# A two-layer hybrid encoder on one core: gate rows through device memory, idle transposes with another term order, and roots by logarithm and exponential

## The chip, the cores and the metric

The kernel runs on one core of a Trainium2 chip. The metric is the time on the device in microseconds (us); lower is better. Before the change the median of three runs is 829.52 us (829.41 to 829.79). A core has five engines that run at the same time, each with its own list of instructions in a fixed order: TensorE (PE in the profile: matrix products and transposes, with its weight loads as PEld), VectorE (DVE), ScalarE (ACT: functions such as exponential, also plain copies), GpSimd (POOL) and SyncE (SP, which here only issues transfers). SyncE and ScalarE each issue transfers (DMAs) on a queue of their own. Data lies in device memory, in the on-chip memory of 128 partitions, and in eight accumulation banks that TensorE writes.

## The reference, cut to what matters

The sequence has 512 tokens of width 1024, all in 32-bit floats. Both layers have one frame; only the mixers differ.

```
ada = silu(c) @ ada_w + ada_b                  # one vector of 3072 for each layer
shift, scale, gate = split(ada, 3)
h = rmsnorm(x, norm_g) * (1 + scale) + shift   # rmsnorm: x * rsqrt(mean(x*x) + 1e-6) * g
... = split(h @ in_w)                          # layer 0: a, u, v, gate path; layer 1: q, k, v and more
y = concat(mixer 1, mixer 2) * silu(gate path)
x = x + gate * (y @ out_w)                     # the "gate row" is this vector gate, 1024 long
```

Layer 0 mixes by causal pooling and by a spatial gating; layer 1 by gated linear attention and by stick-breaking attention. A last `rmsnorm` ends the program.

## The kernel before, in words

**Precision.** Each 32-bit operand of a large product is split into a rounded high part (copied by ScalarE, line 185 or 190) and the remainder (subtracted by VectorE, line 186 or 191). `mm3` (lines 198 to 201) adds three products: high by high, high by low, low by high. A weight tile is 128x1024; four buffers take it raw, three take its two parts, and its load is issued by SyncE.

**Layout.** Activations `x` stand with tokens on the partitions, four blocks of 128 tokens. `h` is kept transposed, features on the partitions: eight tiles `h_hi`, `h_lo` of 128x512. Six of the eight accumulation banks have the tag "mm" and take the large products, two have the tag "aux".

**ada.** `ada_block` multiplies 128 rows of the transposed `ada_w` by `silu(c)` and sums along the row, so that one column of the tile `ada` (128x48) holds 128 values. Columns 16 to 23 of a layer's 24 are the gate.

**First phase.** `prepare_first` makes the norm of the four token blocks of `x`, transposes the first 128 features of each block (line 409) and makes the first `h` tile. After the transposes of blocks 1 to 3 `idle_work` runs 4 transposes of the identity each into a bank that is overwritten later (line 399). Then comes a loop over the eight feature tiles k. Each k has seven products, four for `v` (tokens on the partitions) and three for the gate path, which accumulate in seven banks over all k. For k = 0 all first terms are issued, then the preparation of the next `h` tile, then the second and third terms; for the others the three terms of a product follow each other. `prepare(k + 1)` transposes (line 314, in `modulate`), scales and splits the next `h` tile. After the loop `tok_evac` copies the `v` banks out (lines 466 and 468), and the next unit of products begins in the banks that become free.

**Gate rows.** The last product of a layer has tokens on the partitions, so the gate must lie along the row, the same in every partition, in a tile `gbc` of 128x1024 (line 354 multiplies by it). `gate_half` makes half of it: for four columns of `ada` VectorE spreads the column over a 128x128 tile `rep` (line 327), TensorE transposes it into an "aux" bank (line 332), and ScalarE copies the bank to `gbc` (line 333). For layer 0 `gate_rows(0)` stands ahead of the output product; for layer 1 the halves are set into the steps of the stick-breaking heads.

**Output product and norm.** `out_proj` makes the left 512 columns for all four token blocks, then the right 512 for blocks 0 and 1, and then for 2 and 3. Each evacuation multiplies by `gbc`, adds `x`, and lets ScalarE sum the squares of the half row (`square`, line 343) into a column of `ss`. After the first half it calls `mid`, after each pair of blocks `after`. In layer 0 `after` is `ln1`: `token_rstd` adds the two half sums on VectorE (line 369), GpSimd turns the sum into the mean (line 299) and raises it to the power -0.5 (line 300), and VectorE multiplies the block by the root (`normalise`, line 305); TensorE's transposes of the next layer's `modulate` wait for it. In layer 1 `after` is `final`, which already takes the root as exp(-0.5 ln(...)) on ScalarE (lines 969 and 970), with the first half's mean as the logarithm's bias. The function table for both is loaded in `mid`.

**Order.** A planner orders each engine's instructions by readiness, program order first among those that are ready, and adds the waits; it may start work far ahead of its place in the program. Where the code says `manual_schedule`, the named engine keeps the program's order: all three engines in `prepare_first`, TensorE in the first phase and in the attention part of layer 1, where `at` and `boundary` hang small pieces of work into the gaps between quarter units. Tiles of one tag are handed out in turn: "big" has five buffers of 128x1024, which the tiles `v`, `gbc`, `n`, `gv`, `sv` and `fg` share.

Of the kernel before, what the change touches and what calls it, by code (L numbers as in the profile page):

```python
# [9 lines left out]
F32 = mybir.dt.float32  # L10
F32R = mybir.dt.float32r
AF = mybir.ActivationFunctionType
ALU = mybir.AluOpType
PSUM = bass.MemoryType.PSUM

D = 1024
# [23 lines left out]
def pack_inputs(i):  # L40
# [12 lines left out]
    ng, ab = np.asarray(i["norm_g"]), np.asarray(i["ada_b"])  # L53
# [22 lines left out]
    for c in range(4):  # L76
# [6 lines left out]
        "adaT": f(np.asarray(i["ada_w"]).transpose(0, 2, 1).reshape(48, P, D)),  # L83
# [15 lines left out]
def trunk(ctx: ExitStack, tc: tile.TileContext, d, out):  # L99
# [5 lines left out]
    psum = ctx.enter_context(tc.tile_pool(name="psum", bufs=1, space=PSUM))  # L105
    uid = [0]
# [214 lines left out]
    def gate_half(l, n):  # L321

        reps = []
        for i in range(4):
            c = 24 * l + 16 + 4 * n + i
            reps.append(pool.tile([P, P], F32, name=nm("rep"), tag="diag", bufs=4))
            V.tensor_scalar(out=reps[i], in0=ones, scalar1=ada[:, c:c + 1], scalar2=None, op0=ALU.mult)

        def turn(g):
            ps = bank("aux")  # L330
            for i in range(4):
                T.transpose(ps[:, i * P:(i + 1) * P], reps[i], ident)
            A.copy(out=g[:, n * 512:(n + 1) * 512], in_=ps)
        return turn

    def gate_rows(l):
        g = big("gbc")
        for n in range(2):
            gate_half(l, n)(g)
        return g  # L340
# [4 lines left out]
    def out_proj(wo, y, gbc, ssc, after, mid, nxt):  # L345
# [19 lines left out]
        return late  # L365

# [34 lines left out]
    def prepare_first():  # L401
# [4 lines left out]
        for t in range(TB):  # L406
            if t == TB - 1:
                last_block(0, P)
            T.transpose(ps[:, t * P:(t + 1) * P], xn[t][:, :P], ident)
            idle_work(t and 4)  # L410
# [23 lines left out]
    with tc.manual_schedule(engines={T.engine}):  # L434
        with tc.manual_schedule(engines={V.engine, A.engine}):
            prepare_first()
        for k in range(KT):
            ops = list(first_products(k))
            if k:
                if k + 1 < KT:  # L440
                    prepare(k + 1)
                for o in ops:
                    mm3(*o, False, k == KT - 1)
                continue
            for ps, lh, ll, rh, rl in ops:
                T.matmul(ps, lh, rh, start=True, stop=False)
            prepare(1)
# [4 lines left out]
            for ps, lh, ll, rh, rl in ops[:TB]:  # L452
                T.matmul(ps, ll, rh, start=False, stop=False)
            for ps, lh, ll, rh, rl in ops[TB:]:
                T.matmul(ps, lh, rl, start=False, stop=False)
# [140 lines left out]
    def ln1(tbs):  # L596
        xn = {t: normalise(t, token_rstd(t, 16)) for t in tbs}

        def late():
            for k in range(KT):  # L600
                modulate(1, k, tbs, xn)
        return late
    pre = []

    def preload():
        pre.append(tc.keep_in_program_order(A.preload_act_table_set("natural_log_exp_and_others")))
# [300 lines left out]
    gbc, turns = big("gbc"), []  # L907
    wo1 = stream(d["wo1"])
    at(g0 + 2, lambda: turns.append(gate_half(1, 0)))
    at(g0 + 3, lambda: turns[0](gbc))  # L910
    at(g0 + 3, lambda: turns.append(gate_half(1, 1)))
    at(g0 + 5, lambda: turns[1](gbc))
# [43 lines left out]

    fg = big("fg")
    nc.sync.dma_start(out=fg, in_=d["fg"].to_broadcast([P, D]))

    def first_sum(t):  # L960

        s = sm("msq")
        V.tensor_scalar(out=s, in0=ss[:, 24 + 2 * t:25 + 2 * t], scalar1=1.0 / D, scalar2=EPS, op0=ALU.mult, op1=ALU.add)
        return s

    def final(tbs):
        for t in tbs:
            r = sm("rstd")
            A.activation(out=r, in_=ss[:, 25 + 2 * t:26 + 2 * t], func=AF.Ln, scale=1.0 / D, bias=msq[t])
            A.activation(out=r, in_=r, func=AF.Exp, scale=-0.5)  # L970
# [8 lines left out]
    msq = [None] * TB  # L979

    def scale_first():
        tc.keep_in_program_order(A.preload_act_table_set("natural_log_exp_and_others"))
        for t in range(TB):
            msq[t] = first_sum(t)
# [21 lines left out]
```

## Time and profile before

| What | Value |
|---|---|
| median of three runs | 829.52 us |
| the profiled execution's own time | 829.61 us |
| its span (first to last instruction) | 827.9 us |
| TensorE busy | 812.4 us, 98% of the span |
| VectorE busy | 510.1 us, 62% |
| ScalarE busy | 401.7 us, 49% |
| GpSimd busy | 55.0 us, 7% |
| moved by DMA | 108.50 MB, mean 131 GB/s |
| ScalarE's table loads | 4, of 1.28 us each |

A row of the timeline gives the start in us from the span's start, the duration, the engine, the line of the kernel, the operation, the tile written and the tiles read, shapes and the count of merged instructions. In brackets at its end stands how long the engine had been idle before it, and what released it. Matmuls overlap: the next one starts before the one before has ended, so their pace is read from starts. TensorE's transposes are listed as matmuls that read `ident`. A row of a group gives shortest, median and longest duration in ns and the first and the last start. A row of the DMA issues gives KB each and the us from issue to landing.

### The profile page before, as it was taken

To read this page: it belongs to the slowest core of one execution; us is meant where nothing else is said; L and a number is where in the kernel's file an instruction comes from. 1 tells how busy PE (TensorE), PEld (TensorE's weight loads), DVE (VectorE), ACT (ScalarE), POOL (GpSimd) and SP (SyncE) were. 2 spreads that over 40 slices of the span, in tenths; PEclk is the share of its full clock that TensorE was granted. 3 is DMA by queue.
4 is the path that set the end of the run, shared out by engine and by line. 5 is a ranking of instruction groups with operands and counts; after the bars stand their busy time and mean duration, and the time that the engine had idled before them with its cause. 6 is when DMAs were issued, how large, how long until landed. Compare 5 with 4: busy or idle time off the path is not lost.

```text
span 827.9 us, 9967 instructions
## 1 busy us (share of the span) xinstructions
PE 812.4 (98%) x3696; PEld 663.3 (80%) x3696; DVE 510.1 (62%) x806; ACT 401.7 (49%) x675; POOL 55.0 (7%) x122
## 2 busy tenths in 40 slices
PE   6999999999999999999999999999999999999996
PEld 4888888888888888778888888877777777888885
DVE  6856855588783377744664543475756568434885
ACT  5453321233243265653453423666767668552663
POOL 3000301100000000000000000011010101020000
PEclk9999999999999999999999999999999999999999
DMA  8977555554552235423222121222121212322362
GB/s 301 303 284 236 192 174 170 198 178 155 176 203 80 95 116 178 164 97 102 88 91 72 69 90 51 103 82 96 50 80 51 99 55 77 102 77 96 108 201 105
DMA packets 31298, 108.50 MB, mean 131 GB/s; under 512 B 3601, under 2 KB 3729, under 8 KB 31250
## 3 DMA queue, kind: packets, MB, share of 16 engines
q1 hardware_dynamic: 30674, 106.82, 38.5%
q10 hardware_dynamic: 576, 1.05, 0.3%
q8 instruction: 29, 0.48, 0.2%
q14 instruction: 19, 0.16, 0.1%
HBM read 105.76 MB, written 2.10 MB: 130 GB/s over the span
## 4 chain that ended last, share of the span: by engine, by line
PE 95%; DVE 2%; DMA 1%; ACT 1%; issue 1%; POOL 0%; SPq 0%; DVEq 0%; ACTq 0%
PE mm L200 27%; PE mm L201 27%; PE mm L199 27%; PE aux L848 2%; PE aux L883 2%; PE aux L875 1%; PE aux L529 1%; PE aux L759 1%; PE aux L314 1%; DMA x<-in_x 1%; PE aux L761 1%; PE aux L201 1%; PE aux L199 1%; PE aux L200 1%; PE aux L732 1%; PE aux L770 1%
## 5 line engine op out<-in xcount | busy, mean ns | idle before, releaser
L186 DVE TENSOR_TENSOR wlo<-raw,whi 128x1024 fp32r<-128x1024 f32 (+1 forms) x145 | 178.0, 1228 | 122.5 <-ACT whi L185 122.1
L185 ACT ACTIVATE whi<-raw 128x1024 fp32r<-128x1024 f32 (+1 forms) x145 | 152.4, 1051 | 205.7 <-PE mm L200 93.5
L199 PE MATMUL mm<-hhi,whi 128*128 128x512 f32 x566 | 229.7, 406 | 0.0
L201 PE MATMUL mm<-hhi,wlo 128*128 128x512 f32 x566 | 221.3, 391 | 0.0
L200 PE MATMUL mm<-hlo,whi 128*128 128x512 f32 x566 | 220.9, 390 | 0.0
L200 PEld LDWEIGHTS mm<-hlo,whi 128*128 128x128 f32 x566 | 106.6, 188 | 22.5 <-issue 1.9
L201 PEld LDWEIGHTS mm<-hhi,wlo 128*128 128x128 f32 x566 | 106.3, 188 | 22.8
L199 PEld LDWEIGHTS mm<-hhi,whi 128*128 128x128 f32 x566 | 106.5, 188 | 22.4 <-issue 1.9
L175 DVE CUSTOM_DVE_ANT_0 raw<-raw,sc,cols 128x1024 f32<-128x1024 f32 x48 | 61.4, 1283 | 47.1 <-DMA raw<-in_adaT 46.9
L199 PE MATMUL mm<-whi,hhi 128*128 128x512 f32 x188 | 75.8, 403 | 0.0
L201 PE MATMUL mm<-whi,hlo 128*128 128x512 f32 x188 | 73.9, 393 | 0.0
L200 PE MATMUL mm<-wlo,hhi 128*128 128x512 f32 x188 | 73.6, 391 | 0.0
L201 PE MATMUL mm<-whi,r 128*128 128x512 f32 x160 | 62.7, 392 | 0.0
L199 PE MATMUL mm<-whi,r 128*128 128x512 f32 x160 | 62.5, 392 | 0.0
L200 PE MATMUL mm<-wlo,r 128*128 128x512 f32 x160 | 62.5, 391 | 0.0
L201 PEld LDWEIGHTS mm<-whi,hlo 128*128 128x128 f32 x188 | 35.3, 188 | 7.5
L190 ACT ACTIVATE r<-y 128x256 fp32r<-128x256 f32 (+1 forms) x60 | 27.0, 479 | 29.2 <-PE mm L201 23.2
L191 DVE TENSOR_TENSOR r<-y,r 128x256 fp32r<-128x256 f32 (+1 forms) x60 | 29.1, 510 | 19.4 <-PE mm L200 16.5
L200 PEld LDWEIGHTS mm<-wlo,hhi 128*128 128x128 f32 x188 | 35.4, 188 | 6.9
L199 PEld LDWEIGHTS mm<-whi,hhi 128*128 128x128 f32 x188 | 35.4, 188 | 6.7
L200 PEld LDWEIGHTS mm<-wlo,r 128*128 128x128 f32 x160 | 30.1, 188 | 6.4 <-DVE wlo L186 0.3
L199 PEld LDWEIGHTS mm<-whi,r 128*128 128x128 f32 x160 | 30.1, 188 | 6.1
(222 smaller groups left out, 1052.4 us busy)
## 6 DMA issues: line engine op xcount, KB each, us to landing
raw<-in_w SPq DMA_DIRECT2D x89, 512.0 KB, 3.3
raw<-in_adaT SPq DMA_DIRECT2D x48, 512.0 KB, 4.3
raw<-in_wo SPq DMA_DIRECT2D x48, 512.0 KB, 3.3
raw<-in_wfirst SPq DMA_DIRECT2D x8, 448.0 KB, 4.4
x<-in_x SPq DMA_DIRECT2D x4, 512.0 KB, 5.3
kq<-in_poolw SPq DMA_DIRECT2D x4, 256.0 KB, 5.8
out<-x SPq DMA_DIRECT2D x4, 256.0 KB, 2.6
out<-x ACTq DMA_DIRECT2D x4, 256.0 KB, 2.8
```

The source lines that it names most:

```text
L175: V.tensor_tensor_reduce(out=t, in0=t, in1=sc, scale=1.0, scalar=cols[:, C_AB[l] + b:C_AB[l] + b + 1], op0=ALU.mult, op1=ALU.add, accum_ou ...
L185: A.activation(out=hi[:, :w], in_=t[:, :w], func=AF.Copy)
L186: V.tensor_tensor(out=lo[:, :w], in0=t[:, :w], in1=hi.bitcast(F32)[:, :w], op=ALU.subtract)
L190: A.activation(out=hi, in_=src, func=AF.Copy)
L191: V.tensor_tensor(out=lo, in0=src, in1=hi.bitcast(F32), op=ALU.subtract)
L199: T.matmul(o, lh, rh, start=start, stop=False)
L200: T.matmul(o, lh, rl, start=False, stop=False)
L201: T.matmul(o, ll, rh, start=False, stop=stop)
L314: T.transpose(ps[:, i * P:(i + 1) * P], xn[t][:, k * P:(k + 1) * P], ident)
L529: T.matmul(ps[:, t * P:(t + 1) * P], v[t][:, hd * P:(hd + 1) * P], sguw[hd // 4][:, c], start=True, stop=True)
L848: T.matmul(ps[:, c0:c0 + (t + 1) * P], q[:, t * P:(t + 1) * P], k[:, :(t + 1) * P], start=True, stop=True)
L883: T.matmul(ps[:, s * P:], sv[hd // 4][s][:, hd % 4 * P:(hd % 4 + 1) * P], wt[s], start=s == 0, stop=s == 3)
```

## The change

Three edits are made together.

Gate rows: `gate_half` goes. `gate_rows` stores the eight gate columns of `ada` to a row of device memory and loads that row into all partitions of `gbc`, both on ScalarE's queue. So that the store is contiguous in each partition, the host lays the gate rows of `ada_w` and `ada_b` in another order (`ada_rows`). The steps in the stick-breaking part go, and layer 1 calls `gate_rows(1)` after it.

First phase: `idle_work` runs 6, 7, 9 and 6 transposes after the transposes of blocks 0 to 3, where it ran 0, 4, 4 and 4; and all k use the order of terms that k = 0 had.

Second norm: `ln1` uses `quick_rstd`, the code of `final`, in place of `token_rstd`; `half_means` makes the first half's means of all four blocks in one instruction, for both layers.

```diff
+    def ada_rows(w):
+        return np.concatenate([w[:2 * D], w[2 * D:].reshape(P, 8, -1).transpose(1, 0, 2).reshape(D, -1)])
...
+    dram = ctx.enter_context(tc.tile_pool(name="dram", bufs=1, space=bass.MemoryType.DRAM))
...
-    def gate_half(l, n):
-        reps = []
-        for i in range(4):
-            c = 24 * l + 16 + 4 * n + i
-            reps.append(pool.tile([P, P], F32, name=nm("rep"), tag="diag", bufs=4))
-            V.tensor_scalar(out=reps[i], in0=ones, scalar1=ada[:, c:c + 1], scalar2=None, op0=ALU.mult)
-        def turn(g):
-            ps = bank("aux")
-            for i in range(4):
-                T.transpose(ps[:, i * P:(i + 1) * P], reps[i], ident)
-            A.copy(out=g[:, n * 512:(n + 1) * 512], in_=ps)
-        return turn
-
     def gate_rows(l):
         g = big("gbc")
-        for n in range(2):
-            gate_half(l, n)(g)
+        row = dram.tile([1, D], F32, name=nm("grow"))
+        c = ada[:, 24 * l + 16:24 * l + 24]
+        nc.scalar.dma_start(out=row.rearrange("o (p n) -> (o p) n", n=8), in_=c)
+        nc.scalar.dma_start(out=g, in_=row.to_broadcast([P, D]))
         return g
...
+    def half_means(ssc):
+        m = sm("msq", TB)
+        V.tensor_scalar(out=m, in0=ss[:, ssc:ssc + 2 * TB:2], scalar1=1.0 / D, scalar2=EPS, op0=ALU.mult, op1=ALU.add)
+        return m
+
+    def quick_rstd(t, ssc, m):
+        r = sm("rstd")
+        A.activation(out=r, in_=ss[:, ssc + 2 * t + 1:ssc + 2 * t + 2], func=AF.Ln, scale=1.0 / D, bias=m[:, t:t + 1])
+        A.activation(out=r, in_=r, func=AF.Exp, scale=-0.5)
+        return r
...
-            idle_work(t and 4)
+            idle_work((6, 7, 9, 6)[t])
...
             ops = list(first_products(k))
-            if k:
-                if k + 1 < KT:
-                    prepare(k + 1)
-                for o in ops:
-                    mm3(*o, False, k == KT - 1)
-                continue
+            if 0 < k < KT - 1:
+                prepare(k + 1)
             for ps, lh, ll, rh, rl in ops:
-                T.matmul(ps, lh, rh, start=True, stop=False)
-            prepare(1)
+                T.matmul(ps, lh, rh, start=k == 0, stop=False)
+            if k == 0:
+                prepare(1)
             for ps, lh, ll, rh, rl in ops[:TB]:
                 T.matmul(ps, lh, rl, start=False, stop=False)
             for ps, lh, ll, rh, rl in ops[TB:]:
                 T.matmul(ps, ll, rh, start=False, stop=False)
             for ps, lh, ll, rh, rl in ops[:TB]:
-                T.matmul(ps, ll, rh, start=False, stop=False)
+                T.matmul(ps, ll, rh, start=False, stop=k == KT - 1)
             for ps, lh, ll, rh, rl in ops[TB:]:
-                T.matmul(ps, lh, rl, start=False, stop=False)
+                T.matmul(ps, lh, rl, start=False, stop=k == KT - 1)
...
-        xn = {t: normalise(t, token_rstd(t, 16)) for t in tbs}
+        xn = {t: normalise(t, quick_rstd(t, 16, means[0])) for t in tbs}
...
     def preload():
-        pre.append(tc.keep_in_program_order(A.preload_act_table_set("natural_log_exp_and_others")))
+        means.append(half_means(16))
+        tc.keep_in_program_order(A.preload_act_table_set("natural_log_exp_and_others"))
...
-    at(g0 + 2, lambda: turns.append(gate_half(1, 0)))
-    at(g0 + 3, lambda: turns[0](gbc))
-    at(g0 + 3, lambda: turns.append(gate_half(1, 1)))
-    at(g0 + 5, lambda: turns[1](gbc))
...
+    gbc = gate_rows(1)
     fg = big("fg")
...
-            r = sm("rstd")
-            A.activation(out=r, in_=ss[:, 25 + 2 * t:26 + 2 * t], func=AF.Ln, scale=1.0 / D, bias=msq[t])
-            A.activation(out=r, in_=r, func=AF.Exp, scale=-0.5)
+            r = quick_rstd(t, 24, means[1])
```

More of the change, by code (lines that the diff above doesn't have):

```diff
@@ L51, in c_tiles @@
         return w[:, c0:c0 + 256].reshape(k, 4, P, 256).transpose(0, 2, 1, 3).reshape(k, P, 1024)
-    ng, ab = np.asarray(i["norm_g"]), np.asarray(i["ada_b"])
+    def ada_rows(w):
+        return np.concatenate([w[:2 * D], w[2 * D:].reshape(P, 8, -1).transpose(1, 0, 2).reshape(D, -1)])
+    ng, ab = np.asarray(i["norm_g"]), [ada_rows(b[:, None])[:, 0] for b in np.asarray(i["ada_b"])]
     cols = np.concatenate(
@@ L82, in pack_inputs @@
         "cols": f(cols),
-        "adaT": f(np.asarray(i["ada_w"]).transpose(0, 2, 1).reshape(48, P, D)),
+        "adaT": f(np.stack([ada_rows(w.T) for w in np.asarray(i["ada_w"])]).reshape(48, P, D)),
         "wfirst": f(first),
@@ L602, in ln1 @@
         return late
-    pre = []
+    means = []
     def preload():
-        pre.append(tc.keep_in_program_order(A.preload_act_table_set("natural_log_exp_and_others")))
+        means.append(half_means(16))
+        tc.keep_in_program_order(A.preload_act_table_set("natural_log_exp_and_others"))
     late = out_proj(d["wo0"], [y[i] for i in Y_ORDER[0]], gbc, 16, ln1, preload, stream(d["wo0"]))
@@ L906, in trunk @@
     g0 = gap[0]
-    gbc, turns = big("gbc"), []
     wo1 = stream(d["wo1"])
-    at(g0 + 2, lambda: turns.append(gate_half(1, 0)))
-    at(g0 + 3, lambda: turns[0](gbc))
-    at(g0 + 3, lambda: turns.append(gate_half(1, 1)))
-    at(g0 + 5, lambda: turns[1](gbc))
     at(g0 + 60, wo1.prime)
@@ L955, in trunk @@
     order.close()
+    gbc = gate_rows(1)
     fg = big("fg")
     nc.sync.dma_start(out=fg, in_=d["fg"].to_broadcast([P, D]))
[L960 to L964, printed above, removed]
     def final(tbs):
         for t in tbs:
-            r = sm("rstd")
-            A.activation(out=r, in_=ss[:, 25 + 2 * t:26 + 2 * t], func=AF.Ln, scale=1.0 / D, bias=msq[t])
-            A.activation(out=r, in_=r, func=AF.Exp, scale=-0.5)
+            r = quick_rstd(t, 24, means[1])
             V.tensor_tensor(out=x[t][:, 512:], in0=x[t][:, 512:], in1=fg[:, 512:], op=ALU.mult)
@@ L977, in final @@
         return lambda: None
-    msq = [None] * TB
     def scale_first():
         tc.keep_in_program_order(A.preload_act_table_set("natural_log_exp_and_others"))
+        means.append(half_means(24))
         for t in range(TB):
-            msq[t] = first_sum(t)
             V.tensor_tensor(out=x[t][:, :512], in0=x[t][:, :512], in1=fg[:, :512], op=ALU.mult)
```

## The prediction

> **What bounds the kernel now.** I read the page's chain of waits first, to see which engine sets the end, then the timeline at the four places that the change touches.
>
> ```profile
> span 827.9 us, 9967 instructions
> ```
> ```profile
> PE 95%; DVE 2%; DMA 1%; ACT 1%; issue 1%; POOL 0%; SPq 0%; DVEq 0%; ACTq 0%
> ```
>
> Nineteen twentieths of the chain are TensorE's own work. So a step counts in one of two ways: it takes instructions out of TensorE's stream, or it ends one of the few waits of TensorE. VectorE, ScalarE and the DMA queues count only where TensorE stands waiting for them. The profiled execution took 829.61 us, 1.71 us more than its span and 0.09 us above the median of the runs (829.52); the sum is made against 829.61.
>
> **Gate rows, what is removed.** Before, `gate_rows` and `gate_half` make each gate row by 8 copies on VectorE, 8 transposes on TensorE and 2 copies out on ScalarE, for both layers. Only the transposes stand on the path.
>
> ```profile
> L332 PE MATMUL aux<-ident,rep x16: 271/273/330, 256.4 to 529.5; 128*128 128x128 f32 x16
> ```
> ```profile
> 256.09 0.39 PE L199 MATMUL mm<-whi,kq 128*128 128x512 f32 x1
> ...
> 259.24 0.40 PE L199 MATMUL mm<-whi,kq 128*128 128x512 f32 x1
> ```
> ```profile
> 522.97 0.39 PE L792 MATMUL aux<-r,ones_r 128*128 128x512 f32 x1
> ...
> 523.87 0.40 PE L200 MATMUL mm<-hlo,whi 128*128 128x512 f32 x1
> ```
>
> Matmuls overlap, so I price by starts and not by durations; 0.227 us is the start-to-start time of a full-size matmul (worked out below). Layer 0: from 256.09 to 259.24 start 9 matmuls and 8 transposes in 3.15 us. Nine matmuls alone take 9 x 0.227 = 2.04, so the transposes cost 1.11 us. Layer 1: from 522.97 to 523.87 start 2 matmuls and 4 transposes in 0.90 us, so 0.90 - 0.45 = 0.45 us; the other four, at 529, cost the same, together 0.90. The term is 1.11 + 0.90, **-2.0 us**. Its bounds are four groups at 0.45, 1.8, and 2.1 with the slower matmuls just behind the groups.
>
> **Gate rows, what is added.** Each layer gets two DMAs on ScalarE's queue: a store of the 128x8 gate columns to device memory, and a load that spreads the row over all partitions. The load reads what the store writes, so ScalarE has to wait for the store between the two, and all ScalarE work placed behind the load waits with it: the rounded weight copies (line 185), which VectorE's line 186 needs, which TensorE needs. The load needs a free "big" buffer, too.
>
> ```profile
> out<-x ACTq DMA_DIRECT2D x4, 256.0 KB, 2.8
> fg<-in_fg SPq DMA_DIRECT2D x1, 512.0 KB, 4.3
> ```
> ```profile
> 800.71 0.38 ACTq L976 DMA_DIRECT2D out<-x  x1
> ```
> ```profile
> 268.31 1.06 ACT L185 ACTIVATE whi<-raw 128x1024 fp32r<-128x1024 f32 x1 [4.38 <-PE mm L201]
> ```
> ```profile
> L327 DVE TENSOR_SCALAR rep<-ones,ada x16: 277/281/288, 69.6 to 524.7; 128x128 f32<-128x128 f32 x16
> ```
>
> An issue costs ScalarE 0.38 us. No DMA of 32 bytes a partition is in the trace; the nearest store is the output's, 2.8 us to landing, and I take that, with 0 (landed long before) and twice it, 5.6, as ends. The load has the shape of `fg`, 4.3 us. If store and load are adjacent, ScalarE stands 0.38 + 2.8 + 0.38 = 3.6 us; ends 0.8 and 6.4. At the first place its cover is the 4.38 us for which ScalarE waits for TensorE before each weight copy, and behind that two more finished weight buffers of three. I expect the wait itself to be mostly absent: the planner starts ready work early (the L327 row: the first `rep` copy ran at 69.6, though its place in the program is at 256), and the store is ready as soon as the last gate column is computed, long before a "big" buffer falls free for the load. Even at their place in the program, issue, store, issue and load end 0.38 + 2.8 + 0.38 + 4.3 = 7.9 us later, in the second of the eight weight tiles that go before line 354 reads the row. The new row order in `ada_rows` is host packing; the VectorE and ScalarE copies that fall away were off the path. Term: 0, ends 0 and +6.4 for each layer if the cover is gone; what is late next is then a weight copy, and TensorE behind it.
>
> **First phase: idle transposes.** Line 399 runs 12 transposes into a bank that is overwritten; the change makes it 6, 7, 9 and 6, so 28, and the first six stand where there were none.
>
> ```profile
> 9.22 1.06 PE L399 MATMUL mm<-ident 128*128 128x128 f32 x4
> 11.27 0.47 PE L409 MATMUL aux<-ident,n 128*128 128x128 f32 x1 [0.99 <-DVE n L305]
> ...
> 14.98 2.04 PE L446 MATMUL mm<-whi,hhi 128*128 128x512 f32 x4 [0.24 <-DVE hhi L412]
> ...
> 20.68 1.07 PE L453 MATMUL mm<-whi,hlo 128*128 128x512 f32 x4
> ...
> 22.62 0.48 PE L199 MATMUL mm<-whi,hhi 128*128 128x512 f32 x1
> ```
>
> Four idle transposes take 1.06, the last alone 0.42, so one starts every (1.06 - 0.42)/3 = 0.213 us. The 0.99 us wait behind the second group holds 4 more, so seven fit where four are now, and 28 about fill all gaps before 14.98. A group that overruns its gap holds up the next real transpose by one start at most, by my estimate, 0.2 us. What they may do is wake TensorE's clock: at 20.68 a matmul starts every (1.07 - 0.39)/3 = 0.227 us, but from 14.98 to 20.68 start 14 matmuls and 4 transposes in 5.70 us, where 14 x 0.227 + 0.45 = 3.63 would do. If the clock is up at 14.98, 2.07 us are to be had.
>
> TensorE can't keep them, for the next unit waits for other engines.
>
> ```profile
> 56.27 1.06 ACT L185 ACTIVATE whi<-raw 128x1024 fp32r<-128x1024 f32 x1 [0.27 <-DMA raw<-in_w]
> 57.24 0.57 ACT L468 COPY v<-mm 128x512 f32<-128x512 f32 x1
> ```
> ```profile
> 58.49 0.39 PE L199 MATMUL mm<-whi,hhi 128*128 128x512 f32 x1
> ```
>
> All six "mm" banks are in use, so the next unit's first matmul, at 58.49, needs the bank that the copy at 57.24 empties at 57.81; this copy stands behind a weight copy that waits for a DMA, and DMA doesn't get faster. The gain is cut to 58.49 - 57.81, about 0.65 us. Ends: 0.2 slower (the clock stays down, and the idle groups overfill their gaps) and 2.07 faster (the copy is placed ahead). I take **-0.65 us**, since only a planner's other order would lift the cap.
>
> **First phase: term order.** In `for k in range(KT)` every k now gets all its first products, then the second and third, as k = 0 had it. The count is the same. It moves the first need of `hlo` from the third matmul of a k to the fifteenth.
>
> ```profile
> 21.53 0.69 DVE L319 TENSOR_TENSOR hlo<-silu,hhi 128x512 fp32r<-128x512 f32 x1
> ```
>
> Now `hlo` of k = 1 is ready at 22.22 and wanted at 22.62 + 0.32 + 0.23, so the order is worth nothing by itself. With the clock up early, k = 1 starts near 20.55, and the old order would wait some 1.1 us. It protects the gain and has no term of its own. It also ends the `v` banks within the final seven matmuls of k = 7: without the faster clock the first bank's last matmul would start at 58.49 - 7 x 0.227 = 56.90, and the copy at 57.24 would find it all but full.
>
> **Second norm.** In `ln1` the chain sum (VectorE), two GpSimd instructions, `normalise` becomes logarithm and exponential on ScalarE, with the first half's mean formed ahead in `half_means`.
>
> ```profile
> 346.17 0.19 ACT L343 ACTIVATION_READ_ACCUMULATOR junk<-x 128x1 f32 x1
> 346.27 1.05 ACT L185 ACTIVATE whi<-raw 128x1024 fp32r<-128x1024 f32 x1
> 347.47 1.06 ACT L185 ACTIVATE whi<-raw 128x1024 fp32r<-128x1024 f32 x1 [0.16 <-ACT whi L185]
> ```
> ```profile
> 351.74 0.19 ACT L343 ACTIVATION_READ_ACCUMULATOR junk<-x 128x1 f32 x1
> ```
> ```profile
> 348.02 0.75 DVE L305 TENSOR_SCALAR n<-x,rstd 128x1024 f32<-128x1024 f32 x1 [0.94 <-POOL rstd L300]
> ```
> ```profile
> 348.92 0.30 PE L314 MATMUL aux<-ident,n 128*128 128x128 f32 x1 [0.63 <-DVE n L305]
> ```
> ```profile
> 354.07 0.33 PE L314 MATMUL aux<-ident,n 128*128 128x128 f32 x1 [0.38 <-DVE n L305]
> ```
>
> TensorE waits 0.63 us for block 2 and 0.38 for block 3. The same pair of functions already runs in `final`:
>
> ```profile
> 797.39 0.18 ACT L343 ACTIVATION_READ_ACCUMULATOR junk<-x 128x1 f32 x1
> 797.49 1.05 ACT L185 ACTIVATE whi<-raw 128x1024 fp32r<-128x1024 f32 x1
> 798.44 0.28 ACT L969 ACTIVATE rstd<-ss,msq 128x1 f32<-128x1 f32 x1
> ...
> 798.93 0.19 ACT L970 ACTIVATE rstd<-rstd 128x1 f32<-128x1 f32 x1
> ```
> ```profile
> 818.44 0.19 ACT L343 ACTIVATION_READ_ACCUMULATOR junk<-x 128x1 f32 x1
> ```
> ```profile
> 818.99 0.20 ACT L970 ACTIVATE rstd<-rstd 128x1 f32<-128x1 f32 x1
> ```
>
> Undisturbed, the root is there 818.99 + 0.20 - 818.44 = 0.75 us after the accumulator read; with a weight copy in between, 798.93 + 0.19 - 797.39 = 1.73. Now `normalise` starts 348.02 - 346.17 = 1.85 after it. Block 3 has no weight copy behind it, so its wait goes: -0.4. Block 2 has two: between the wait gone (-0.6) and the exponential behind both (+0.8) I take -0.3, as the planner starts what is ready and of these the root comes first in the program. Blocks 0 and 1 look like the 797 rows and change nothing. Term **-0.7 us**, ends -1.0 and +0.4. In `final`, the pair is the same as before and three small VectorE instructions fall away, under TensorE's matmuls: 0.
>
> **Sum:** 829.61 - 2.0 - 0.65 - 0.7 = 826.26; against the median 826.2.
>
> **Rivals.** *The clock stays down* (chance 0.18): the first phase does not do what it says. For it: the 12 present transposes are followed by slow matmuls; against it: they leave gaps such as the 0.99 us before 11.27. Time 829.6 - 2.7 = 826.9. The Trainium skill, page "TensorE: Matmul & The Clock Gate", Part 4, speaks for this one: it says that transposes don't count as busy for the clock gate in the way matmuls do. By that rule the time is the same 826.9; the trace neither proves nor refutes it, since its idle transposes are interrupted. Part 1 of that page has the gate judge windows of 3.4 us; by that, with transposes counted, the clock would be up before 14.98.
>
> *No cap* (0.09): the planner puts the bank's copy first. Then 2.07 instead of 0.65, 824.8. Against it: the copy stands behind two weight copies now.
>
> *The roots queue* (0.10): the exponential stands behind both copies at 346.27 and 347.47. The norm costs +0.4 instead of -0.7, 827.3. For it: the 797 rows.
>
> *ScalarE stands at the store* (0.16): store and load adjacent, at a place where the cover is gone, that is, where ScalarE owes TensorE something within 3.6 us, as in the norm at 346 to 356. Exposed once (0.08) 826.2 + 3.6 = 829.8, no change; exposed in both layers (0.08) 833.4, slower. Against it: the early store. It decides from the point where the wait passes 4.4 us beside weight copies, or at once in the norm, where TensorE waits already. The Trainium skill, "DMA: Bandwidth & Descriptors", section "Two DMAs through the same engine are not ordered", says that a DMA which reads what an earlier one wrote has to wait for that one's semaphore at the issuing engine; no row of before shows such a pair.
>
> **How the numbers follow.** The forecast has 0.45; a rest of 0.02 I count as no change. A measurement of this kernel tells some 0.2%, 1.7 us, from none. Faster: 0.45 + 0.18 + 0.09 + half of the queueing roots (0.5 us from the bound), 0.05, is 0.77. No change: 0.05 + 0.08 + 0.02 = 0.15. Slower: 0.08. The range goes from 824.5 (no cap, with the upper end of the gate rows) to 829.8 (one exposure).
>
> **What would show it.** Gate rows: no L332 rows, four more ScalarE DMA issues, and TensorE without wait near 256 and 523. Clock: starts 0.227 us apart from 14.98. Cap: a TensorE wait for line 468 before the next unit. Norm: no wait at block 3, a smaller one at block 2. A TensorE wait for weight copies behind the new DMAs, or a start later than 14.98, would make the forecast wrong.

## The result, and the profile after

The changed kernel took 825.01 us (median of 4 runs, 823.95 to 826.16) beside 829.64 us before (4 runs): a ratio of 0.9947, with a 95% interval of 0.9935 to 0.9959. The forecast was 826.2 us. The profiled execution took 825.07 us, 4.54 us less than that of before; its span is shorter by as much (827.89 to 823.35). One execution of a kernel further down, norm_late, took 2923.46 us and is left out of the ratio given there.

The span and the chain of waits on the page of the changed kernel, then its new DMA issues (KB each, median us from issue to landing):

```profile
span 823.3 us, 9948 instructions
...
PE 88%; DMA 5%; DVE 3%; ACT 1%; issue 1%; POOL 1%; SPq 0%; DVEq 0%; ACTq 0%
```

```profile
gbc<-grow ACTq DMA_DIRECT2D x2, 512.0 KB, 5.1
...
grow<-ada ACTq DMA_DIRECT2D x2, 4.0 KB, 4.7
```

TensorE had 95% of the chain and has 88%. The rest is a stretch at the start, where the chain now runs through landings of weights and VectorE. TensorE's waits say where; first all of them (us in total, times, longest), then the timeline of the first phase and of the gating matmuls:

```profile
PE aux L161 <- ACT c_row L157: 3.6, 1, 3.6
PE mm L204 <- ACT v L471: 1.0, 1, 1.0
PE aux L532 <- DVE v L507: 0.7, 1, 0.7
PE mm L448 <- DVE hhi L418: 0.3, 1, 0.3
```

```profile
10.94 2.13 PE L405 MATMUL mm<-ident 128*128 128x128 f32 x9
12.86 0.42 PE L415 MATMUL aux<-ident,n 128*128 128x128 f32 x1
13.08 0.86 PE L405 MATMUL mm<-ident 128*128 128x128 f32 x6
14.28 1.17 PE L448 MATMUL mm<-whi,hhi 128*128 128x512 f32 x4 [0.34 <-DVE hhi L418]
...
55.61 0.39 PE L458 MATMUL aux<-hlo,whi 128*128 128x512 f32 x1
56.97 0.50 PE L204 MATMUL mm<-whi,hhi 128*128 128x512 f32 x1 [0.97 <-ACT v L471]
...
91.33 1.38 PE L532 MATMUL aux<-kq,v 128*128 128x128 f32 x10 [0.74 <-DVE v L507]
```

Nine idle transposes take 2.13 us from 10.94, six take 0.86 from 13.08, so the pace has doubled by then (the trace's record of the full clock starts at 13.16 us; the last section says how to read it), and the first four products at 14.28 take 1.17 where they took 2.04. TensorE ends the phase 2.65 us earlier than before (its last matmul at 55.61 against 58.26). It keeps little of that: it waits 0.97 us for the copy that empties the first bank (line 471, the 468 of before), as forecast, and again at 91.33, where the gating matmuls need the last block of `v` from VectorE. There it is only 0.47 us ahead. That is less than the 0.70 us by which the first product came sooner in this execution (14.28 against 14.98), where the third block of `x` had landed 0.86 us sooner (7.48 against 8.34).

The waits of the norm are gone from the list, and so are both transposing steps of the gate rows. The norm of block 2, on ScalarE, VectorE and TensorE:

```profile
344.01 1.05 ACT L190 ACTIVATE whi<-raw 128x1024 fp32r<-128x1024 f32 x1
344.96 0.28 ACT L369 ACTIVATE rstd<-ss,msq 128x1 f32<-128x1 f32 x1
345.14 1.05 ACT L190 ACTIVATE whi<-raw 128x1024 fp32r<-128x1024 f32 x1
346.10 0.18 ACT L370 ACTIVATE rstd<-rstd 128x1 f32<-128x1 f32 x1
...
346.84 0.74 DVE L310 TENSOR_SCALAR n<-x,rstd 128x1024 f32<-128x1024 f32 x1
...
347.73 0.41 PE L319 MATMUL aux<-ident,n 128*128 128x128 f32 x2
```

The exponential does stand behind both weight copies, in the order that one rival had, and yet TensorE doesn't wait: its transposes come at 347.73, behind matmuls of the next unit that the planner has put ahead of them. At block 3 it doesn't wait either.

The two transfers of each layer and ScalarE's work behind the second store:

```profile
101.36 0.36 ACTq L331 DMA_DIRECT2D grow<-ada  x1
...
146.47 0.33 ACTq L332 DMA_DIRECT2D gbc<-grow  x1
...
240.08 0.36 ACTq L331 DMA_DIRECT2D grow<-ada  x1
240.57 1.06 ACT L190 ACTIVATE whi<-raw 128x1024 fp32r<-128x1024 f32 x1 [7.62 <-DVE ada L180]
...
502.69 0.33 ACTq L332 DMA_DIRECT2D gbc<-grow  x1
```

In both layers the store stands far ahead of its load, so no load waits for it. ScalarE does stand, though, 7.62 us ahead of 240.57: the second store had been put where its last gate column wasn't summed yet. TensorE doesn't wait for it.

To compare kernels stage by stage I number TensorE's matmuls from the first product on, without those that read `ident`; they are the same in all kernels but for the order of terms in the first phase. The 1st to 15th hold the slow stretch, the 169th begins the next unit; the 397th starts at 104 to 107 us, the 1297th at 304 to 308, the 1597th at 377 to 383. Each row is worked out from the starts in one trace, in us:

| kernel | 1st at | 1st to 15th | 15th to 169th | 169th to 397th | 397th at | 397th to 1297th | 1297th to 1597th | 1597th to last |
|---|---|---|---|---|---|---|---|---|
| before | 14.98 | 5.70 | 37.81 | 48.03 | 106.52 | 201.49 | 74.69 | 437.41 |
| after | 14.28 | 3.75 | 38.94 | 49.22 | 106.19 | 200.35 | 72.67 | 436.44 |
| gates_alone | 14.28 | 5.27 | 37.81 | 48.02 | 105.38 | 200.35 | 74.66 | 436.45 |
| norm_alone | 14.04 | 4.55 | 39.30 | 48.82 | 106.71 | 201.50 | 72.67 | 437.41 |
| first_alone | 14.79 | 3.76 | 38.47 | 48.33 | 105.35 | 201.49 | 74.67 | 437.43 |
| all_again | 14.07 | 3.74 | 37.89 | 48.02 | 103.72 | 200.35 | 72.69 | 436.48 |
| idle_alone | 14.93 | 3.75 | 39.29 | 48.03 | 106.00 | 201.50 | 74.67 | 437.43 |
| order_alone | 14.38 | 5.48 | 37.80 | 48.03 | 105.69 | 201.50 | 74.67 | 437.43 |
| copy_first | 15.04 | 3.76 | 38.01 | 48.02 | 104.83 | 200.35 | 72.69 | 436.46 |
| copy_and_fill | 15.09 | 3.75 | 38.25 | 48.74 | 105.83 | 200.35 | 72.66 | 436.48 |
| norm_late | 14.56 | 6.02 | 37.83 | 48.02 | 106.43 | 201.49 | 73.05 | 437.41 |
| store_late | 15.11 | 3.76 | 38.33 | 49.07 | 106.27 | 200.35 | 72.69 | 436.45 |
| light_before | 13.54 | 4.79 | 38.23 | 48.03 | 104.59 | 201.50 | 74.70 | 437.41 |
| light_first | 14.12 | 3.79 | 37.80 | 48.03 | 103.74 | 201.50 | 74.69 | 437.41 |

The three columns at the right repeat to 0.04 us among kernels that share an edit. So the gate rows are worth 201.50 - 200.35 + 437.41 - 436.45 = 2.11 us and the second norm 74.68 - 72.67 = 2.01 us. The columns at the left don't repeat: up to the 397th matmul, kernels without the first-phase edit and with all loads lie between 105.38 and 106.71, those with both parts of it between 103.72 and 106.27.

### The profile page after: what moved, and what is told of

Its sections match the earlier page's. It is cut to its first block, busy times and chain, and to the rows that moved or that the text cites. A ratio compares the mean times of both kernels' runs of the same rounds, so it can differ in the third digit from the quotient of the medians.

```text
span 823.3 us, 9948 instructions
## 1 busy us (share of the span) xinstructions
PE 810.2 (98%) x3696; PEld 662.9 (81%) x3696; DVE 506.2 (61%) x784; ACT 399.9 (49%) x679; POOL 52.0 (6%) x114
## 3 DMA queue, kind: packets, MB, share of 16 engines
q10 hardware_dynamic: 1152, 2.11, 0.7%
HBM read 106.81 MB, written 2.11 MB: 132 GB/s over the span
## 4 chain that ended last, share of the span: by engine, by line
PE 88%; DMA 5%; DVE 3%; ACT 1%; issue 1%; POOL 1%; SPq 0%; DVEq 0%; ACTq 0%
PE mm L206 25%; PE mm L204 25%; PE mm L205 25%; PE aux L852 2%; PE aux L887 2%; DMA raw<-in_wfirst 2%; DMA raw<-in_adaT 2%; DVE wlo L191 1%; DVE raw L180 1%; PE aux L879 1%; DMA raw<-in_w 1%; PE aux L763 1%; PE aux L532 1%; PE aux L765 1%; PE aux L736 1%
## 5 line engine op out<-in xcount | busy, mean ns | idle before, releaser
L204 PE MATMUL mm<-hhi,whi 128*128 128x512 f32 x552 | 223.9, 406 | 0.0
L206 PE MATMUL mm<-hhi,wlo 128*128 128x512 f32 x552 | 215.6, 391 | 0.0
L205 PE MATMUL mm<-hlo,whi 128*128 128x512 f32 x552 | 215.2, 390 | 0.0
L205 PEld LDWEIGHTS mm<-hlo,whi 128*128 128x128 f32 x552 | 103.8, 188 | 22.3 <-issue 1.9
L204 PE MATMUL mm<-whi,hhi 128*128 128x512 f32 x160 | 64.5, 403 | 1.0 <-ACT v L471 1.0
L205 PE MATMUL mm<-wlo,hhi 128*128 128x512 f32 x160 | 62.6, 391 | 0.0
L206 PE MATMUL mm<-whi,hlo 128*128 128x512 f32 x160 | 62.6, 391 | 0.0
L204 PEld LDWEIGHTS mm<-whi,hhi 128*128 128x128 f32 x160 | 30.1, 188 | 7.3 <-ACT v L471 1.4
L206 PEld LDWEIGHTS mm<-whi,hlo 128*128 128x128 f32 x160 | 30.0, 188 | 6.4
L206 PEld LDWEIGHTS mm<-whi,r 128*128 128x128 f32 x160 | 30.1, 188 | 6.1
L204 PEld LDWEIGHTS mm<-whi,r 128*128 128x128 f32 x160 | 30.0, 188 | 6.2
```

Source lines behind the costliest of these rows:

```text
L204: T.matmul(o, lh, rh, start=start, stop=False)
L205: T.matmul(o, lh, rl, start=False, stop=False)
L206: T.matmul(o, ll, rh, start=False, stop=stop)
```

## The experiments

### The three parts alone, and all again

Each part was put into the kernel before by itself, in the lines of the diff above (the gate rows with their packing, the second norm with `final`'s joined function, the first phase with both its edits); all_again is the changed kernel once more.

> The kernel before with the gate rows through memory alone (with the packing that they need). Theory from the two traces: the transposes that fall away are worth 2.1 us (starts around 256 and 523 to 529), and nothing waits for the store or the load, so 2.1 us faster than before, with an interval no wider than that of before (its median runs lie within 0.4 us), because the first phase is as before. Prediction's sizes: 2.0 faster. Rival, ScalarE stands at the store: less than 1 us faster, and a TensorE wait for weight copies just behind the place of the DMAs.

> The kernel before with the second norm's roots by logarithm and exponential alone (and the joined functions in the last norm). Theory from the two traces: 2.0 us faster, all of it between 320 and 360 us, in small steps: a weight remainder that VectorE no longer makes late, and the transposes of blocks 2 and 3 without wait. Prediction's sizes: 0.7 us faster, 0.6 of block 2's and 0.4 of block 3's wait less what queues. Rival, roots queue behind weight copies: 0 to 0.4 us slower. The runs spread as before, some 0.4 us.

> The kernel before with the 28 idle transposes and the term order of the first phase alone. Theory from the two traces: the clock is up at the first product and TensorE is 2 to 2.6 us ahead at the end of the phase, but gives back more than 1 us at the copy of the first bank (near 57) and almost 1 us at the gating matmuls that wait for v (near 91); net 0.2 to 1.0 us faster, with runs spread over 1 to 2 us, since the start is now set by DMA landings. Prediction's sizes: 0.65 faster, given back at the first place alone. Rival, no cap: 2.07 us faster. Rival, the clock stays down: 0.

> The changed kernel once more, on the same chip as its three parts. If the parts don't touch each other, its gain is the sum of theirs: by the traces 2.1 + 2.0 + 0.4 = 4.5 us; by the prediction's sizes 3.35 us. If the parts overlap (one hides what another saves), it gains less than the sum, if one opens what another can't use alone, more. Its runs spread over some 2 us if the first phase makes the spread.

| kernel | median us | ratio to before | 95% interval |
|---|---|---|---|
| before | 829.30 | | |
| gates_alone | 826.48 | 0.9967 | 0.9956 to 0.9979 |
| norm_alone | 827.32 | 0.9975 | 0.9966 to 0.9985 |
| first_alone | 828.37 | 0.9989 | 0.9980 to 0.9998 |
| all_again | 824.00 | 0.9934 | 0.9922 to 0.9947 |

The parts add: 0.33 + 0.25 + 0.11 = 0.69% against 0.66% for all. The gate rows' time shows 2.8 us (interval 1.7 to 3.6), but of its trace only 2.11 us belong to the edit (the table); up to the 397th matmul that execution is 1.1 us ahead of the one of before, in a first phase that the edit doesn't touch. The norm's 2.0 us agrees with its stage. The first phase gains 0.9 us, with an interval from 0.2 to 1.7, so the prediction's 0.65 fits and the 2.07 of the uncapped start doesn't. In first_alone's own trace it isn't the cap that takes the rest. The next unit begins at 57.02 without a wait, and the loss, 0.62 us, is at the first product of k = 2 (26.36): the transposes ahead of it wait for ScalarE's scaling, which stands behind a weight copy whose load landed late (the copy, at 24.02, had waited 3.75 us).

My expectation that only the edited first phase spreads its runs was wrong: before itself spread over 828.44 to 830.73 on this chip, gates_alone over 2.7 us. The changed kernel itself gained 4.6 us in the first comparison and 5.3 us in this one; differences below some 0.7 us between two comparisons tell nothing.

all_again shows the start without any cap. Its chain and the place where the changed kernel's first trace waited:

```profile
PE 97%; DVE 1%; DMA 1%; ACT 0%; SPq 0%; issue 0%; POOL 0%; DVEq 0%; ACTq 0%
```

```profile
52.05 1.06 ACT L190 ACTIVATE whi<-raw 128x1024 fp32r<-128x1024 f32 x1 [2.96 <-DMA raw<-in_w]
53.39 1.06 ACT L190 ACTIVATE whi<-raw 128x1024 fp32r<-128x1024 f32 x1 [0.28 <-DMA raw<-in_w]
54.53 1.08 ACT L471 COPY v<-mm 128x512 f32<-128x512 f32 x2
...
55.47 0.39 PE L458 MATMUL aux<-hlo,whi 128*128 128x512 f32 x1
55.70 0.39 PE L204 MATMUL mm<-whi,hhi 128*128 128x512 f32 x1
```

The weight tile landed in time for 52.05, where it was 54.05 in the first trace of the same program. The copy stood ready and TensorE went on in its usual 0.23 us. So whether the cap bites depends on landings that differ between executions.

### Idle transposes and term order, each alone

```diff
 # idle_alone: before with
-            idle_work(t and 4)
+            idle_work((6, 7, 9, 6)[t])
 # order_alone: before with the loop over k of the changed kernel
```

> The kernel before with the 28 idle transposes alone, each k after the first still in the old order (three products of one bank in a row). Prediction: the old order wants hlo of k = 1 at its third matmul and would wait some 1.1 us there, so the idle transposes alone gain less than both edits together (0.9 us measured), by up to 1.1 us, that is 0 or a little slower than before; the trace shows a TensorE wait for hlo near 21. Rival: what the start gains is taken by DMA landings in any case, so the order makes no difference, and this kernel is 0.9 us faster like both edits together.

> The kernel before with the term order alone, 12 idle transposes as before. Prediction: 0, within 0.3 us of before, for hlo isn't late without the faster clock. Rival: the order is what lets the last banks end within seven matmuls, or moves the copies of the v banks, and gains or loses 0.5 us or more by itself.

Before took 829.13 us in this comparison. idle_alone took 829.12 (ratio 1.0002, 0.9993 to 1.0012), order_alone 829.10 (1.0000, 0.9991 to 1.0009). Neither shows a gain alone (the intervals reach from 0.6 us faster to 1.0 slower, and 0.75 us either way); together they gain 0.9 us (0.2 to 1.7). The timeline of idle_alone shows a reason:

```profile
14.93 1.17 PE L446 MATMUL mm<-whi,hhi 128*128 128x512 f32 x4 [0.59 <-DVE hhi L412]
...
20.94 0.40 PE L200 MATMUL mm<-wlo,hhi 128*128 128x512 f32 x1
22.32 0.50 PE L201 MATMUL mm<-whi,hlo 128*128 128x512 f32 x1 [0.98 <-DVE hlo L319]
```

The fast pace is there from 14.93. Then the third matmul of k = 1 waits 0.98 us for `hlo`; the prediction had put some 1.1 us on it. In the table idle_alone gains 1.95 us up to the 15th matmul and gives back 1.48 by the 169th, 1.14 of it at this matmul. norm_alone, where the pace rose early of itself (4.55), gives back 1.49 there, 0.8 of it at two waits for `hlo`. With the new order as well, the six traces with all loads give back 0.1 to 1.1 us there, none of it in a wait for `hlo`.

### The two places that cap the start

copy_first takes the changed kernel and sets ScalarE's first copy of a `v` bank ahead of the next unit's second weight copy; copy_and_fill also holds VectorE's filler reductions, from the fourth on, behind the last scaling of `v`.

```diff
+    tiles = [nxt()]
+    copy = A.copy(out=v[0][:, :512], in_=v_ps[0])
+    with tc.issue_after(copy.ins):
+        tiles.append(nxt())
...
+            with tc.issue_after(norms[-1].ins):    # copy_and_fill only
+                fill.pop(0)()
```

> The changed kernel with ScalarE's first copy of a v bank placed ahead of the second rounded weight copy of the next unit, and ScalarE's other copies and silu behind it. If the cap that the prediction named (the copy behind a weight copy that waits for a DMA) costs time in the end, the wait of TensorE for that copy near 57 goes and the kernel is 0.5 to 1.1 us faster than the changed kernel of this call's conditions (5.3 us faster than before), so 5.8 to 6.4 us faster than before. If what is gained there is given back at the gating matmuls near 91, which wait for the last v, or is never lost in most runs, it stays at 5 to 5.5 us. If the second weight tile is now late, it loses 0.5 us or more.

> As copy_first, and the reductions of the gate weights that VectorE does between, from the fourth on, queued behind the last scaling of v, so that the root of the last block doesn't stand behind one of them (1.28 us each). If that second place caps the gain of the start, the gating matmuls near 91 no longer wait and start 0.7 to 1.0 us earlier, and the kernel gains as much over copy_first. If the start is paced by the landings of weights rather than by the order on VectorE, it is within 0.3 us of copy_first, or slower, since four reductions hold their buffers longer.

```profile
53.99 1.06 ACT L192 ACTIVATE whi<-raw 128x1024 fp32r<-128x1024 f32 x1 [2.60 <-DMA raw<-in_w]
55.65 0.59 ACT L497 COPY v<-mm 128x512 f32<-128x512 f32 x1 [0.59 <-PE mm L458]
56.13 1.06 ACT L192 ACTIVATE whi<-raw 128x1024 fp32r<-128x1024 f32 x1
...
56.81 0.39 PE L206 MATMUL mm<-whi,hhi 128*128 128x512 f32 x1
```

In copy_first the tile lands as late (53.99) as in the first trace of the changed kernel, and TensorE doesn't wait at 56.81. But it also comes there 1.0 us later than in that trace (its last product of the phase starts at 56.58 against 55.61), so the trace doesn't settle whether the order lifts the cap. The time doesn't show it either: 823.70 us against 829.13 (ratio 0.9936, 0.9923 to 0.9948), the same as all_again's 0.9934. In copy_and_fill there is no wait at the gating matmuls; but there is none in copy_first and all_again either, so that isn't shown to come from the fillers. TensorE loses 0.3 us at its first matmul of the next unit (the first weight copy waited for its load until 55.51, and the bank copy behind it ended at 57.03) and 0.6 at the second, which waits for a weight remainder from VectorE (0.79 us from start to start); 824.14 us, ratio 0.9939 (0.9926 to 0.9951). Both places are real in a trace, but not in every one. Of the seven traces that have both edits of the first phase, the first place costs 1.1 us in the first and 0.2 to 0.3 in two more; the second costs 0.9 us in the first and 0.75 in store_late. What they cost on the median is below what these runs can tell. Neither kernel is better than the changed one by more than that.

### Less to load

The 16 tiles of `ada_w` that the first phase reads (they give the shift and the scale of layer 0, though the expectations call them gate weights) were loaded and reduced over a quarter of their columns, 6 MB less, in the kernel before and in first_alone. Both kernels leave out three quarters of each of these sums.

```diff
-        t = raw(d["adaT"][n])
+        w = 256 if l == 0 and b < 16 else D
+        t = raw(d["adaT"][n][:, :w], w)[:, :w]
```

> The kernel before with the 16 gate weight tiles of the first phase loaded and reduced over a quarter of their columns only (leaves out three quarters of each sum), so that 6 MB of loads fall away where DMA is busiest. The pair for light_first. If TensorE's clock and x alone set the start, no faster than before by more than 0.3 us; if landings hold the start up, faster by 0.5 us or more.

> Both first-phase edits (28 idle transposes and the term order) over light_before. Theory, landings: what keeps the two edits from their 2 us is the landing of weights in the first 60 us; with 6 MB less to load they gain 1.7 to 2.7 us over light_before, where they gained 0.9 us with all loads. Rival, the cap by the order of ScalarE's and VectorE's work (the bank copy near 57, the last v near 91): the gain over light_before stays at 0.7 to 1.0 us. If the clock were all, the gain is the same in both pairs.

light_before took 828.40 us (ratio 0.9990, 0.9981 to 0.9998), 0.8 us less than before (0.2 to 1.6), so loads and reductions do hold up the old start. light_first took 827.08 (0.9974, 0.9963 to 0.9984), 1.3 us less than light_before. That lies between both expectations: more than 0.9, less than 1.7. light_first's trace has the undisturbed 37.80 and 48.03 of the table and reaches the 397th matmul at 103.74, as all_again did with all loads. The 0.4 us between the gains of the two pairs, 1.3 and 0.9, is less than the intervals allow to tell, so that late landings take part of the gain is seen in traces (first_alone, and the first of the changed kernel) and not shown by the time. What does show is that the slow stretch the edit removes isn't always as long as in the profile of before: without the edit it took 4.55 to 6.02 us in six traces, which leaves 0.8 to 2.3 us over the 3.75, not 2.07 each time.

### A later root

```diff
+        for _ in range(extra):        # 4 in the second norm
+            A.copy(out=r, in_=r)
         A.activation(out=r, in_=r, func=AF.Exp, scale=-0.5)
```

> The second norm's roots alone (as norm_alone, 2.0 us faster than before), with four extra copies of 128x1 on ScalarE between logarithm and exponential, so that each root of the second norm is some 1.2 us later: about as long from the accumulator read to the scaling as the old chain over GpSimd (1.85 us). Theory, length of the chain: the gain comes from the shorter chain, so TensorE waits again, above all for blocks 2 and 3, and at least 1 us of the 2.0 is lost. Rival, who does it: the planner knows ScalarE's times and puts the transposes later, behind other matmuls, and VectorE no longer stands for GpSimd with weight remainders queued behind; then at least 1.5 of the 2.0 us stay.

norm_late took 827.75 us against 829.19 (ratio 0.9978, 0.9969 to 0.9987); its stage takes 73.05 us, so 1.63 of the 2.01 us stay. Block 2 in its timeline:

```profile
345.67 0.19 ACT L343 ACTIVATION_READ_ACCUMULATOR junk<-x 128x1 f32 x1
...
347.87 0.84 ACT L378 COPY rstd<-rstd 128x1 f32<-128x1 f32 x4
348.74 0.20 ACT L379 ACTIVATE rstd<-rstd 128x1 f32<-128x1 f32 x1
...
350.32 0.75 DVE L305 TENSOR_SCALAR n<-x,rstd 128x1024 f32<-128x1024 f32 x1
...
351.21 0.41 PE L314 MATMUL aux<-ident,n 128*128 128x128 f32 x2
```

The scaling starts 350.32 - 345.67 = 4.65 us after the accumulator read, where before it was 1.85, and TensorE has no wait in its list for it: the planner put the transposes and VectorE's scaling later. Here the chain is longer than GpSimd's was, and only 0.4 us of the gain go; so 1.6 us don't hang on its length. They come with the chain on ScalarE and the orders that the planner then gives VectorE and TensorE; no run separates the two, for instance by keeping GpSimd's chain and putting the transposes later. That the planner's figure for GpSimd's part was too short in the kernel before would explain the misfit; no run tests that figure either.

### The store right ahead of its load

```diff
-    gbc = gate_rows(0)
+    with tc.issue_after(whis[-1].ins):    # the last weight copy of the pool part
+        gbc = gate_rows(0)
```

> The changed kernel with the first layer's store and load of the gate row queued behind the last weight copy of the pool part, so that ScalarE comes to the load (near 243) with the store only just issued, one copy between. The store lands 3.6 to 6.6 us after its issue in the changed kernel, so ScalarE stands 3 to 6 us. Prediction: the cover there (ScalarE waits of 4 us ahead of each weight copy, and finished weight buffers) hides it: no TensorE wait, within 0.3 us of the changed kernel (5.3 us faster than before). Rival, ScalarE stands at the store with the cover gone: a TensorE wait for a weight copy or for a rounded y, and 1 to 4 us of the 5.3 lost.

```profile
239.79 0.36 ACTq L333 DMA_DIRECT2D grow<-ada  x1
240.27 1.06 ACT L192 ACTIVATE whi<-raw 128x1024 fp32r<-128x1024 f32 x1 [6.78 <-DVE ada L180]
240.30 0.33 ACTq L333 DMA_DIRECT2D grow<-ada  x1
...
244.81 0.33 ACTq L334 DMA_DIRECT2D gbc<-grow  x1
245.26 1.06 ACT L192 ACTIVATE whi<-raw 128x1024 fp32r<-128x1024 f32 x1 [3.45 <-DMA grow<-ada]
```

ScalarE stands 6.78 us for the other layer's last gate column and, a weight copy and a bank copy later, 3.45 us for the store, together 10 us. (The 3.6 to 6.6 us of the expectation are the ends over stores and loads together; the two stores alone took 4.6 and 4.7 us in the changed kernel, 4.5 and 4.8 here.) TensorE has no wait behind it, and the stage from the 397th to the 1297th matmul takes 200.35 us as in all kernels with the gate rows through memory. The time, 825.17 us (ratio 0.9950, 0.9938 to 0.9962), is 1.2 us above all_again's, more than the 0.3 us expected, but close to the 825.01 us of the changed kernel in the first comparison; the traces differ only ahead of the 397th matmul (106.27 against 103.72), a stretch in which store_late has no store. So the wait is free at this place. The norm, where the prediction feared it most, was not tried.

## Why the prediction was right and where it was not

**Gate rows, removed: right.** The step said -2.0 us with bounds of 1.8 and 2.1; the stages show 2.11, the upper bound, so the slower matmuls just behind the groups count.

**Gate rows, added: right in the sum, wrong in the wait.** The store of layer 0 was early, as expected (101.36), and its load came when a "big" buffer fell free (146.47). But "the wait itself mostly absent" failed for layer 1, where ScalarE stood 7.62 us for the data of the store, not for its landing. The cover was sized too small as well: the rival was to decide from 4.4 us on, and 7.62 us in one stretch cost nothing, nor did the 10 us in two of store_late. The store lands in 4.6 to 4.7 us, where 2.8 was taken from the output's stores and 5.6 was the end.

**Idle transposes: the size fits partly by luck, of the cause one half.** The step took 2.07 us to be had and a cap that leaves 0.65. Both edits of the first phase alone gain 0.9 us (0.2 to 1.7). The pace is up at the first product in all eight traces with 28 idle transposes (3.74 to 3.79 us for the first 15 matmuls), as the step said. The cap stands where the prediction put it in the first trace, but it is missing in all_again and in first_alone; there the gain is less than 2.07 for other reasons, a shorter slow stretch to remove in most executions and weights that land late at other places. That a cap read from one trace gave the right size is luck. What the step didn't have is the spread: it read one length of the slow stretch and one landing of the weights as if they were fixed, and it didn't see the second place, the last block of `v`, at all. The estimate that an overfull group costs 0.2 us holds: in the changed kernel's trace the group of nine, begun at the slow pace, leaves block 3's transpose at 12.86 and the first product at 14.28; in all_again, whose inputs come at the same time, they stand at 12.49 and 14.07.

On the rival that the clock stays down, the trace decides against the rule of the Trainium skill, "TensorE: Matmul & The Clock Gate", Part 4, that transposes don't count as busy, at least for the idle transposes as this kernel issues them: in idle_alone nothing but transposes ran on TensorE from 7.28 to 14.93, the pace doubled within them (nine take 1.15 us from 11.34), and before differs from it by 16 of them alone. Part 1 of the same page of the Trainium skill says that the window runs free of the program, so that the count of slow matmuls differs between runs; the 4.55 to 6.02 us without the edit agree with that, and so do the lengths of the clock's records in the last section.

**Term order: right.** No term of its own, and the wait it avoids was 0.98 us for a predicted 1.1.

**Second norm: mis-sized, and of the cause one half.** The step priced -0.7 (block 3 -0.4, block 2 -0.3, blocks 0 and 1 nothing); it is -2.01. Read along the stage, the gain grows by 0.55 us where VectorE no longer stands for GpSimd in front of a weight remainder (block 0), by 0.27 at block 1 and by 1.20 at blocks 2 and 3. "Blocks 0 and 1 change nothing" looked at ScalarE's rows alone; VectorE's row of the kernel before had the wait and TensorE's the result:

```profile
323.33 0.75 DVE L305 TENSOR_SCALAR n<-x,rstd 128x1024 f32<-128x1024 f32 x1 [0.95 <-POOL rstd L300]
...
325.87 0.50 PE L200 MATMUL mm<-wlo,kq 128*128 128x512 f32 x1 [0.25 <-DVE wlo L186]
```

For block 2 the step added the queueing of the root (+0.8) to the end of the wait, as if TensorE's order stood still; the planner moved the transposes instead. That the waits go was right. The reason given, a root that comes sooner, holds for little of it: in norm_late block 2's root comes 3.27 us after the accumulator read, where with GpSimd even the scaling began after 1.85, and 1.63 of the 2.01 us stay.

**The rest.** `final` was put at 0; norm_alone takes 437.41 us from the 1597th matmul on, as before. Of the sum, -3.35 us, the parts gave -2.11, -2.01 and -0.33 in the profiled execution (up to the 397th matmul, 106.52 to 106.19), together -4.45 of the span's -4.54. The -0.33 is no gain of the first phase in that execution, since its first product came 0.70 us earlier, after an earlier landing of `x`. The forecast was 1.2 us high, nearly all by the norm.

## What to carry to other kernels

Where a planner orders the work, price a shorter chain by asking which engine stands in front of it and what is queued behind that engine, and not by the wait of the last reader alone. A head start at the beginning of a kernel is worth what the next landings and the next in-order queue let through: look two waits further than the first cap, and at more than one trace. A DMA that reads what another wrote cost nothing here, where the issuing engine had slack, and the slack could be measured by moving the pair together.

## What the hardware showed that was not expected

The doubled pace doesn't show in the granted clock of the profile's windows. Two stretches of the kernel before, then one of all_again, as busy time by engine with the count of instructions (PE first); the third figure from the right is the granted clock:

```profile
15.00:19.00 4.00, 4.00 (x12) 3.22 (x13) 3.92 (x7) 1.93 (x3) 0.00 (x0) 1.00 0.87 273
19.00:23.00 4.00, 4.00 (x21) 3.36 (x21) 3.68 (x6) 1.61 (x3) 0.00 (x0) 1.00 0.83 293
```

```profile
14.00:18.00 4.00, 3.93 (x19) 3.32 (x20) 4.00 (x7) 2.01 (x3) 0.00 (x0) 1.00 0.87 307
```

Twelve matmuls in 4 us and 21 in the next 4 us of the kernel before stand beside the same 1.00. But the 1.00 of the first stretch isn't a measurement. The packed trace holds the clock as records, each with a start, a length and a share, and this view counts time without a record as full clock. In every trace here the first record starts some 10 to 20 us into the span, at full clock, and the pace doubles just there: at 19.22 us in before, 13.16 in the first trace of the changed kernel, 10.82 in all_again. In the six traces without the 28 idle transposes it starts at 15.78 to 19.45 us, behind the first product; in the eight with them at 10.07 to 13.44, ahead of it.

The length of the slow stretch follows from that start. Matmuls start 0.427 us apart ahead of it and 0.227 behind it, so each us from the first product to the record's start costs 1 - 0.227/0.427 = 0.47 us. In norm_alone that is 15.78 - 14.04 = 1.74 us, or 0.8 us, and 3.75 + 0.8 is the 4.55 of the table; all six traces come out so within 0.04 us. That its length without the edit differed by 1.5 us between traces is thus a matter of when the clock was granted. The records of full clock last 802.13, 805.55, 808.96 or 812.37 us in the fourteen traces, whole steps of 3.41 us apart. So the clock seems to change on a grid of 3.41 us, and where the program's start falls on that grid would move the change by as much; no run sets that.

A store of 4 KB, 32 bytes from each partition, took longer to land (4.7 us) than the median store of 256 KB at the end of the kernel (2.6 and 2.7 us on the two queues). And a small load of layer 1 (`gl_raw`, 64 KB), whose buffers the gate rows no longer use, moved by itself from 258.4 us up to 60.0, into the busy stretch, where it lands in 5.6 us instead of 1.8; it is first read at 361.3, so no engine waits for it.
